# Opening of a hybrid RWKV-7 / HGRN2 step: clearings moved from GpSimd to VectorE, masks and norm scaling reordered

## The chip, the core and the metric

One core of a Trainium2 chip runs the whole program. The time is device microseconds of one launch, as a median over runs. A profiled execution adds a trace of every instruction: TensorE (PE, with its weight loads PEld), VectorE (DVE), ScalarE (ACT), GpSimd (POOL), SyncE (SP, which here issues the DMAs). Each engine takes its instructions in a fixed order, and an instruction waits for the semaphores of the ones whose results it needs; everything behind it on that engine waits with it.

## The reference, cut to what matters

One decoder layer serves 256 prompt tokens and 8 sequences of 8 sampled tokens, together 320 tokens of width 2048. The part that the change touches is the beginning:

```
h = x * rsqrt(mean(x*x) + eps) * norm_g        # rms_norm, 320 x 2048
p = h @ w_in                                   # 2048 -> 12416 columns
```

From p come the two branches: RWKV-7 (token shift, decay, a delta-rule matrix state for 16 heads) and HGRN2 (a gated linear recurrence for 8 heads, chunk by chunk). Each is projected back to 2048 columns, the two are merged by sigmoid gates computed from p, and an output projection, a residual add and a final norm follow. The states and shift rows are outputs too.

## The kernel before, in words

All large products are done in three passes. Each float32 operand is split in a high part (a cast to the fp32r type) and a low part (what is left), and high x high, low x high and high x low are summed in PSUM. The weights come in blocks of 1024 rows by 128 columns (512 KB, tile `raw`); ScalarE makes the high part `whi`, VectorE or GpSimd subtracts to make the low part `wlo`. There are three buffers of each, so a weight load (SyncE) must wait until the low part of the block three earlier has been taken. The result of one column tile is 128 columns x 320 tokens, 48 matmuls.

The kernel has four parts. The opening loads x, norms it, turns it to 16 tiles of 128 channels x 320 tokens and computes the first column tile of `p`. Then comes a long part whose instructions are recorded and put in an order by a planner with fixed costs (L1448 is the line that issues all of them), then the gates and projections, and the output projection. The change is in the opening alone.

The opening, as the code has it:

- x lies in three tiles `xt`: two of 128 prompt tokens and one of 64 sampled tokens (number 2, loaded first). `norm_g` is loaded as 4 rows of 512 (`gq`).
- Before the hand-ordered part GpSimd prepares constants: `ident`; `gr` and `sel`, which are cleared (L410, L411) and used to spread norm_g; `rows` (L417); the masks `lvs`, `lvz`, `seqm` (L449 to L463), `mk` (L468 to L474) and `mf` (L480 on). The masks are made by clearing and then cutting with affine selects (`keep_ge`, L437). L474 multiplies two 128 x 64 blocks of `mk` by `seqm`, and L494 copies `mf` four times as bytes into `mu8`.
- The rest stands in a part in which PE, ScalarE, VectorE and GpSimd take their instructions exactly as written. VectorE first fills `ones`, the `jr_...` matrices (L551 to L556), `yz`, `qz` and others (L563), `rs_a` and `rs_b`.
- norm_g is spread over 128 partitions: ScalarE casts `gq` into `gr` (L574), VectorE puts the rest in rows 32 to 35 (L575), four matmuls of `sel` and `gr` (L578) give four banks of PSUM, and VectorE copies them into `gb` (L579). VectorE then clears `arp` (L580).
- `warm(n)` issues n matmuls whose result nobody uses (L541).
- For each x tile, ScalarE sums the squares (`squares`, L502) and makes the factor (`scale`, L507 and L508). VectorE multiplies x by factor and norm_g (`gain`, L513) in pieces of 512 or 1024 columns. PE transposes (`turn`, L525) into one of six PSUM buffers, ScalarE takes the high part (`high`, L529), VectorE the low part (`low`, L533), which sets the buffer free.
- `first(part, k4)` issues four matmuls of one of the three passes of the first column tile (L612). `half(b, hf)` splits half of a weight block, ScalarE the high part (L618), GpSimd the low part (L619). `divide` splits a whole one (L401, L402).
- SyncE loads weight block 0 again as soon as `half(0, 1)` is done, block 1 after `half(1, 1)`, block 2 after `divide(2, 1, G)` (all L395).
- At the end ScalarE copies `seq4` and `lvz` (L671 to L673). The first instructions of the planned part then read the first tile's result (`pad`), run the decay's low-rank input through exponentials, and split the weights `wst` and `ast` of a small product that PE needs early.

Of the kernel before, what the change touches and what calls it, by code (L numbers as in the profile page):

```python
# [9 lines left out]
F32 = mybir.dt.float32  # L10
# [284 lines left out]
def hybrid_step(ctx, tc, x_prompt, x_sample, state_rwkv, state_hgrn, state_shift, norm_g, w_in,  # L295
# [4 lines left out]
    V, S, G, T = nc.vector, nc.scalar, nc.gpsimd, nc.tensor  # L300

    S.add_instruction(mybir.InstLoadActFuncSet(
        name=nc.get_next_instruction_name(), act_func_set_id=EXP_LN_SET, ins=[], outs=[]))
# [11 lines left out]
    def ctile(shape, name, dt=F32, pool=rconst):  # L315
        return pool.tile(shape, dt, name=name, tag=name)
# [17 lines left out]
    HS = [slice(0, 64), slice(64, 128)]  # L334
# [41 lines left out]
    with tc.tile_pool(name="start", bufs=1) as st, \  # L376
            tc.tile_pool(name="pst", bufs=6, space=PSUM) as pst:
        gq = st.tile([4, 512], F32, name="gq")
        nc.sync.dma_start(gq, norm_g.rearrange("o (r c) -> (o r) c", c=512))
        gb = st.tile([128, D], F32, name="gb")  # L380
# [17 lines left out]
        def divide(b_, n, sub):  # L398
            for j in range(n):
                ks = slice(8 * j // n, 8 * (j + 1) // n)  # L400
                S.copy(whi[b_][:, ks], wraw[b_][:, ks])  # L401
                sub.tensor_sub(wlo[b_][:, ks], wraw[b_][:, ks], whi[b_][:, ks].bitcast(F32))  # L402
            return whi[b_], wlo[b_]
# [3 lines left out]

        gr = st.tile([64, 512], F32R, name="gr")
        sel = st.tile([64, 4, 128], F32R, name="sel")
        G.memset(gr.bitcast(F32), 0.0)  # L410
        G.memset(sel.bitcast(F32), 0.0)  # L411
        for h in range(2):
            sl = slice(32 * h, 32 * h + 32)
            G.affine_select(out=sel[sl], in_=sel[sl], pattern=[[-1, 4], [0, 128]],
# [29 lines left out]
        low_ = HS[0]  # L444
        lvs = st.tile([128, 5, 32], F32, name="lvs")
        lvz = ctile([128, 5, 2, 32], "lvz")
        seqm = ctile([128, NSEQ], "seqm")
        mk_lv = {}
        G.memset(lvs[low_], 1.0)  # L449
        G.memset(seqm[low_], 1.0)  # L450
        for n, sz in enumerate((2, 4, 8, 16, 32)):
            mk_lv[sz] = lvz[:, n]
# [5 lines left out]
        keep_ge(seqm[low_], [[8, 8]], 7, -1)  # L458

        seq4 = ctile([128, 4], "seq4")  # L460
        G.memset(lvz[low_, :, 1], 0.0)
        G.memset(lvz[HS[1], :, 0], 0.0)
        G.tensor_copy(seqm[HS[1]], seqm[low_])  # L463

        mk = ctile([128, 3, 2, 64], "mk")
        G.memset(mk[:, 0:2], 1.0)  # L468
        for c_ in range(2):
            for sl in HS:  # L470
                keep_ge(mk[sl, c_], [[1, 2], [1, 64]], -1, -1)
# [6 lines left out]
        mf = st.tile([32, 3, 32], F32, name="mf")  # L478
        mu8 = ctile([128, 3, 32], "mu8", U8)
        G.memset(mf, 1.0)  # L480
        for n, sz in enumerate((8, 8, 16)):
# [8 lines left out]
            G.memset(lv[:, :, 0, :], 0.0)  # L490
            keep_ge(lv[:, :, 1, :], [[-2 * sz, nb], [0, sz]], 0, 1)
            keep_ge(lv[:, :, 1, :], [[2 * sz, nb], [0, sz]], sz - 1, -1)
        for g in range(4):
            G.tensor_copy(mu8[32 * g:32 * g + 32], mf)  # L494

        junk = st.tile([128, D], F32, name="junk")
        ssq = [st.tile([128, 2], F32, name=f"ssq{j}") for j in range(3)]

# [11 lines left out]
        def gain(j, k4, w=1):  # L510
            xt, n = xts[j]
            cs = slice(512 * k4, 512 * (k4 + w))
            V.scalar_tensor_tensor(xt[:n, cs], xt[:n, cs], ssq[j][:n, 0:1], gb[:n, cs], op0=ALU.mult, op1=ALU.mult)  # L513
# [13 lines left out]
        def high(j, k4):  # L527
            _, ks, tok = span(j, k4)
            S.copy(hhi[:, ks, tok], tps[j, k4])  # L529

        def low(j, k4):
            _, ks, tok = span(j, k4)
            V.tensor_sub(hlo[:, ks, tok], tps[j, k4], hhi[:, ks, tok].bitcast(F32))  # L533
# [5 lines left out]
        def warm(n):  # L539
            for _ in range(n):  # L540
                T.matmul(wps[:, :256], ones[:, :128], ones, start=True, stop=True)  # L541

        tps = {}
        with tc.manual_schedule(engines={mybir.EngineType.PE, mybir.EngineType.Activation, mybir.EngineType.DVE,
                                        mybir.EngineType.Pool}):
            ones = st.tile([128, 256], F32R, name="ones")
            V.memset(ones.bitcast(F32), 1.0)

            jr_sum, jr_mean, jr_cent, jr_all = (ctile([128, 128], n, F32R)
                                                for n in ("jr_sum", "jr_mean", "jr_cent", "jr_all"))  # L550
            V.memset(jr_all.bitcast(F32), 1.0 / 128.0)  # L551
            for t_, x in ((jr_sum, 1.0), (jr_mean, 1.0 / 64.0)):
                V.memset(t_.bitcast(F32), 0.0)
                for sl in HS:
                    V.memset(t_[sl, sl].bitcast(F32), x)
            V.tensor_sub(jr_cent, ident, jr_mean.bitcast(F32))  # L556

            yz = ctile([128, 2, 2, 2, 64], "yz")
            yd = ctile([128, 2, 2, 64], "yd")
            qz = ctile([128, NSEQ, 32], "qz")  # L560
            arp = ctile([128, 5, 2, 2, 64], "arp")
            for t_ in (yz, qz, lora_lw[HS[1]].bitcast(F32), lora_la[HS[0]].bitcast(F32)):
                V.memset(t_, 0.0)  # L563


            rs_a = ctile([128, NT], "rs_a")
            rs_b = ctile([128, NT], "rs_b")
            V.memset(rs_a, 1.0)
            V.memset(rs_a[:, 0:NP_:64], 0.0)
            V.memset(rs_a[:, NP_::8], 0.0)  # L570
            V.memset(rs_b, 1.0)
            V.memset(rs_b[:, ::8], 0.0)

            S.copy(gr[0:4], gq)  # L574
            V.tensor_sub(gr[32:36], gq, gr[0:4].bitcast(F32))  # L575
            for c_ in range(4):
                ps = pst.tile([128, 512], F32, name="gps", tag="t")
                T.matmul(ps, sel[:, c_], gr, start=True, stop=True)  # L578
                V.tensor_copy(gb[:, 512 * c_:512 * c_ + 512], ps)  # L579
            V.memset(arp, 0.0)  # L580
            warm(16)
            squares(2)
            scale(2)
            gain(2, 0, 2)
            turn(2, 0)
            warm(3)
            gain(2, 2, 2)
            turn(2, 1)
            warm(4)
            squares(0)  # L590
            scale(0)
            gain(0, 0, 2)
            turn(0, 0)
            turn(0, 1)
            squares(1)
            scale(1)
            gain(0, 2, 2)
            gain(1, 0)
            turn(1, 0)
            gain(1, 1)  # L600
            turn(1, 1)
            high(2, 0)
            high(0, 0)
            low(2, 0)
            low(0, 0)
            first_ps = psm.tile([128, 512], F32, name="mps", tag="m")

            def first(part, k4):

                w, x = ((whi, hhi), (whi, hlo), (wlo, hhi))[part]  # L610
                for k_ in range(4 * k4, 4 * k4 + 4):
                    T.matmul(first_ps[:, :NT], w[k4 // 2][:, k_ % 8], x[:, k_], start=part == 0 and k_ == 0,  # L612
                             stop=part == 2 and k_ == KT - 1)

            def half(b_, hf):

                ks = slice(4 * hf, 4 * hf + 4)
                S.copy(whi[b_][:, ks], wraw[b_][:, ks])  # L618
                G.tensor_sub(wlo[b_][:, ks], wraw[b_][:, ks], whi[b_][:, ks].bitcast(F32))  # L619

            half(0, 0)
            high(1, 0)
            low(1, 0)
            first(0, 0)
            gain(1, 2)
            gain(1, 3)
            half(0, 1)
            high(2, 1)
            high(0, 1)
            high(1, 1)  # L630
            low(2, 1)
            low(0, 1)
            low(1, 1)
            turn(0, 2)
            first(0, 1)
            turn(1, 2)
            first(1, 0)
            first(2, 0)
            half(1, 0)
            high(0, 2)  # L640
            high(1, 2)
            low(0, 2)
            low(1, 2)
            turn(0, 3)
            turn(1, 3)
            first(0, 2)
            first(1, 1)
            first(2, 1)
            half(1, 1)
            fetch(0, 0, 1)  # L650
            high(0, 3)
            high(1, 3)
            low(0, 3)
            low(1, 3)
            first(1, 2)
            first(2, 2)
            divide(2, 1, G)
            ps = pst.tile([128, 512], F32, name="cps", tag="t")
            T.transpose(ps[:, :128], rows, ident)
            V.tensor_copy(cols, ps[:, :106])  # L660
            ps = pst.tile([128, 512], F32, name="sps", tag="t")
            for j in range(2):
                T.transpose(ps[:, 100 * j:100 * j + 100], ssr[:, j], ident[:100, :100])
            V.tensor_copy(sst.rearrange("p s r -> p (s r)"), ps[:, :200])
            for part in range(3):
                first(part, 3)
            fetch(1, 1024, 0)
            divide(0, 1, G)
            fetch(2, 1024, 1)
            for j in range(4):  # L670
                S.copy(seq4[32 * j:32 * j + 32], seqm[0:32, 0:4])  # L671
            S.copy(lvz[HS[1], :, 1], lvs[low_])
            S.copy(lvz[low_, :, 0], lvs[low_])  # L673
# [766 lines left out]
    with tc.manual_schedule():  # L1440
# [3 lines left out]
        V, S, G, T, Y = (book.proxy(e) for e in ("V", "S", "G", "PE", "Y"))  # L1444
        record_all()
        V, S, G, T = real
# [193 lines left out]
```

## Time and profile before

| | us |
|---|---|
| median of three runs (1122.93 to 1124.36) | 1123.26 |
| profiled execution | 1123.37 |
| its span, first to last instruction | 1121.7 |
| PE busy | 1102.8 |
| VectorE busy | 761.6 |
| ScalarE busy | 693.1 |
| GpSimd busy | 192.8 |
| first matmul of the planned part (L1448) starts at | 28.98 |

A matmul's end is modelled and matmuls overlap, so PE's busy time is not a measure of PE at its peak. Starts of instructions are better for comparing: where a matmul of 320 columns follows another, they start 0.15 us apart. In rows of the order of time, instructions of one kind that follow each other closely are one row with a count; a row's length is then from the first start to the last end. Spans on GpSimd are rough.

### The profile page before, as it was taken

The numbers are of one execution on the slowest core, as the hardware profiler recorded it, in microseconds if no ns is written. First come the engines' busy times: TensorE is split into PE (matmuls) and PEld (weight loads), VectorE is DVE, ScalarE is ACT, GpSimd is POOL, SyncE is SP. The second block draws the span as 40 slices with busy tenths as digits, with TensorE's granted clock in tenths as the row PEclk, the third lists the DMA queues.
The fourth block names the chain that finished last, engine by engine and source line by source line (L and its number), as shares of the span: only waits on it lengthen the run. The fifth ranks groups of instructions, "written<-read, shape, count | busy, mean of one in ns | idle before, by whom it ended". The sixth has DMA issues, their size and how long they took to land.

```text
span 1121.7 us, 23666 instructions
## 1 busy us (share of the span) xinstructions
PE 1102.8 (98%) x9240; PEld 1066.6 (95%) x9240; DVE 761.6 (68%) x1625; ACT 693.1 (62%) x1572; POOL 192.8 (17%) x411
## 2 busy tenths in 40 slices
PE   6999999999999999999999999999999999999997
PEld 6999999999999999999999999999999999998886
DVE  8778888887887887887887876444444444437532
ACT  6777777677778678677776876444444444435422
POOL 9531231221311411412412200000000000000000
PEclk9999999999999999999999999999999999999998
DMA  6743545435435435435445354555555555587512
GB/s 178 201 132 107 152 117 146 137 98 155 128 96 158 131 105 165 133 96 163 124 124 145 97 144 138 150 150 150 151 149 151 150 151 150 151 269 242 187 33 93
DMA packets 283107, 159.87 MB, mean 143 GB/s; under 512 B 22893, under 2 KB 273264, under 8 KB 282356
## 3 DMA queue, kind: packets, MB, share of 16 engines
q1 hardware_dynamic: 282628, 157.06, 49.0%
q8 instruction: 72, 1.18, 0.4%
q10 hardware_dynamic: 368, 1.31, 0.4%
q14 instruction: 39, 0.32, 0.1%
HBM read 148.53 MB, written 9.81 MB: 141 GB/s over the span
## 4 chain that ended last, share of the span: by engine, by line
PE 94%; POOL 2%; ACT 2%; issue 1%; DVE 1%; DMA 1%; DVEq 0%; ACTq 0%; POOLq 0%
PE mps L1448 41%; PE a L1448 10%; PE mps L361 6%; PE mps L359 6%; PE mps L360 6%; PE b L1448 3%; PE po L1535 3%; PE po L1534 3%; PE po L1533 3%; PE ppa L359 2%; PE ppb L361 2%; PE ppb L359 2%; PE ppa L361 2%; PE ppb L360 2%; PE ppa L360 2%; PE y L1448 1%
## 5 line engine op out<-in xcount | busy, mean ns | idle before, releaser
L1448 PE MATMUL mps<-hhi,whi 128*128 128x320 f32 x1088 | 344.6, 317 | 0.0
L1448 PE MATMUL mps<-hlo,whi 128*128 128x320 f32 x1088 | 344.0, 316 | 0.5 <-issue 0.5
L1448 PE MATMUL mps<-hhi,wlo 128*128 128x320 f32 x1088 | 343.5, 316 | 0.0
L1448 PEld LDWEIGHTS mps<-hhi,whi 128*128 128x128 f32 x1088 | 204.8, 188 | 3.6 <-issue 2.7
L1448 PEld LDWEIGHTS mps<-hlo,whi 128*128 128x128 f32 x1088 | 204.9, 188 | 1.1 <-issue 0.4
L1448 PEld LDWEIGHTS mps<-hhi,wlo 128*128 128x128 f32 x1088 | 204.8, 188 | 0.7
L349 ACT CAST whi<-raw 128x1024 fp32r<-128x1024 f32 x88 | 92.4, 1050 | 162.7 <-PE mps L360 107.3
L350 DVE TENSOR_TENSOR wlo<-raw,whi 128x1024 fp32r<-128x1024 f32 x88 | 107.9, 1226 | 125.0 <-ACT whi L349 124.8
L1448 DVE TENSOR_TENSOR wlo<-raw,whi 128x1024 fp32r<-128x1024 f32 x134 | 164.6, 1228 | 16.9 <-ACT whi L1448 15.5
L1448 ACT CAST whi<-raw 128x1024 fp32r<-128x1024 f32 x134 | 140.2, 1046 | 56.3 <-PE mps L1448 55.3
L359 PE MATMUL mps<-hhi,whi 128*128 128x320 f32 x448 | 138.4, 309 | 0.0
L360 PE MATMUL mps<-hlo,whi 128*128 128x320 f32 x448 | 138.4, 309 | 0.0
L361 PE MATMUL mps<-hhi,wlo 128*128 128x320 f32 x448 | 138.4, 309 | 0.0
L359 PEld LDWEIGHTS mps<-hhi,whi 128*128 128x128 f32 x448 | 84.1, 188 | 0.0
L360 PEld LDWEIGHTS mps<-hlo,whi 128*128 128x128 f32 x448 | 84.1, 188 | 0.0
L361 PEld LDWEIGHTS mps<-hhi,wlo 128*128 128x128 f32 x448 | 84.1, 188 | 0.0
L1522 DVE TENSOR_TENSOR wlo<-raw,whi 128x1024 fp32r<-128x1024 f32 x32 | 38.6, 1223 | 36.9 <-ACT whi L1521 36.7
L1521 ACT CAST whi<-raw 128x1024 fp32r<-128x1024 f32 x32 | 33.2, 1051 | 47.6 <-PE po L1538 22.2
L1448 POOL TENSOR_TENSOR vm<-v,seq 96x512 fp32r<-96x512 f32 x16 | 16.9, 1056 | 200.3 <-ACT uK L1448 152.4
L1535 PE MATMUL po<-wlo,mhi 128*128 128x512 f32 x128 | 50.0, 391 | 0.0
L1533 PE MATMUL po<-whi,mhi 128*128 128x512 f32 x128 | 50.0, 391 | 0.0
L1534 PE MATMUL po<-whi,mlo 128*128 128x512 f32 x128 | 50.0, 391 | 0.0
(439 smaller groups left out, 2244.6 us busy)
## 6 DMA issues: line engine op xcount, KB each, us to landing
raw<-in_w_in_dram SPq DMA_DIRECT2D x194, 512.0 KB
raw<-in_w_out_dram SPq DMA_DIRECT2D x32, 512.0 KB
raw<-in_proj_a_dram SPq DMA_DIRECT2D x16, 512.0 KB
raw<-in_proj_b_dram SPq DMA_DIRECT2D x16, 512.0 KB
s<-in_state_hgrn_dram SPq DMA_DIRECT2D x8, 512.0 KB
out_dram<-s SPq DMA_DIRECT2D x8, 512.0 KB
s<-in_state_rwkv_dram SPq DMA_DIRECT2D x8, 256.0 KB
out_dram<-s SPq DMA_DIRECT2D x8, 256.0 KB
```

The source lines that it names most:

```text
L349: S.copy(hi[:, ks], raw[:, ks])
L350: sub.tensor_sub(lo[:, ks], raw[:, ks], hi[:, ks].bitcast(F32))
L359: T.matmul(dst, hi[:, q, :], xhi[:, k, :], start=(k == 0), stop=False)
L360: T.matmul(dst, hi[:, q, :], xlo[:, k, :], start=False, stop=False)
L361: T.matmul(dst, lo[:, q, :], xhi[:, k, :], start=False, stop=(k == nk - 1))
L1448: o.fn(*o.args, **o.kw)
L1521: S.copy(hi, raw)
L1522: V.tensor_sub(lo, raw, hi.bitcast(F32))
L1533: T.matmul(pt, h, hi, start=first, stop=False)
L1534: T.matmul(pt, l, hi, start=False, stop=False)
L1535: T.matmul(pt, h, lo, start=False, stop=end)
```

## The change

- Six clearings go from GpSimd to VectorE: `gr`, `sel`, `lvs`, two halves of `lvz`, and `mk[:, 0:2]`.
- The four copies of `mf` into `mu8` go from GpSimd to VectorE, behind the last low parts of x and the split of weight block 2.
- The cast and subtraction that make `gr` go to the front of VectorE's and ScalarE's order, right behind `ones`; the four matmuls and the copies to `gb` go right behind `jr_cent`, ahead of the clearings of `yz` and the others. ScalarE does the first and third copy, VectorE the second and fourth.
- The clearing of `arp` goes from in front of the scaling to behind the copies into `mu8`.
- `warm(16)` becomes `warm(20)`.
- `gain(1, 2)` and `gain(1, 3)` go ahead of `low(2, 0)` and `low(0, 0)`, so that all eight pieces of scaling come before the first low part.

```diff
-        G.memset(gr.bitcast(F32), 0.0)
-        G.memset(sel.bitcast(F32), 0.0)
+        V.memset(gr.bitcast(F32), 0.0)
+        V.memset(sel.bitcast(F32), 0.0)
...
-        G.memset(lvs[low_], 1.0)
+        V.memset(lvs[low_], 1.0)
         G.memset(seqm[low_], 1.0)
...
-        G.memset(lvz[low_, :, 1], 0.0)
-        G.memset(lvz[HS[1], :, 0], 0.0)
+        V.memset(lvz[low_, :, 1], 0.0)
+        V.memset(lvz[HS[1], :, 0], 0.0)
         G.tensor_copy(seqm[HS[1]], seqm[low_])
...
-        G.memset(mk[:, 0:2], 1.0)
+        V.memset(mk[:, 0:2], 1.0)
...
-        for g in range(4):
-            G.tensor_copy(mu8[32 * g:32 * g + 32], mf)
...
             V.memset(ones.bitcast(F32), 1.0)
+
+            S.copy(gr[0:4], gq)
+            V.tensor_sub(gr[32:36], gq, gr[0:4].bitcast(F32))
...
             V.tensor_sub(jr_cent, ident, jr_mean.bitcast(F32))
+            for c_ in range(4):
+                ps = pst.tile([128, 512], F32, name="gps", tag="t")
+                T.matmul(ps, sel[:, c_], gr, start=True, stop=True)
+                (V.tensor_copy if c_ % 2 else S.copy)(gb[:, 512 * c_:512 * c_ + 512], ps)
...
-
-            S.copy(gr[0:4], gq)
-            V.tensor_sub(gr[32:36], gq, gr[0:4].bitcast(F32))
-            for c_ in range(4):
-                ps = pst.tile([128, 512], F32, name="gps", tag="t")
-                T.matmul(ps, sel[:, c_], gr, start=True, stop=True)
-                V.tensor_copy(gb[:, 512 * c_:512 * c_ + 512], ps)
-            V.memset(arp, 0.0)
-            warm(16)
+            warm(20)
...
             high(0, 0)
+            gain(1, 2)
+            gain(1, 3)
             low(2, 0)
             low(0, 0)
...
             first(0, 0)
-            gain(1, 2)
-            gain(1, 3)
             half(0, 1)
...
             divide(2, 1, G)
+            for g in range(4):
+                V.tensor_copy(mu8[32 * g:32 * g + 32], mf)
+            V.memset(arp, 0.0)
```

## The prediction

> **What bounds the kernel now.** I read the page first, for the engine that the span belongs to.
>
> ```profile
> PE 1102.8 (98%) x9240; PEld 1066.6 (95%) x9240; DVE 761.6 (68%) x1625; ACT 693.1 (62%) x1572; POOL 192.8 (17%) x411
> PE 94%; POOL 2%; ACT 2%; issue 1%; DVE 1%; DMA 1%; DVEq 0%; ACTq 0%; POOLq 0%
> ```
>
> PE holds 94% of the chain that ended last; the rest is 67 us at most, and the change touches only the first 30 us. So the second view is the list of PE's waits from 29 us to the end, to see whether time saved in the opening can be lost again. These are its two longest rows:
>
> ```profile
> PE a L1448 <- DVE ast L1448: 0.8, 1, 0.8
> PE a L1448 <- DVE pp L1448: 0.7, 2, 0.3
> ```
>
> After 29 us PE waits next to never. Whatever moves the start of its steady stream moves the end by as much, and the first row, one wait of 0.8 us at 38 us, can add to that. The question is therefore when the stream of L1448 starts. The third view is the order of time of the opening, engine by engine (start, length, line, operation, tiles, count; in brackets the idle time and who ended it). VectorE:
>
> ```profile
> 0.93 0.27 DVE L547 MEMSET ones<- 128x256 f32 x1 [0.93 <-PEq L1628]
> 1.18 0.17 DVE L551 MEMSET jr_all<- 128x128 f32 x1
> 2.52 0.68 DVE L556 TENSOR_TENSOR jr_cent<-ident,jr_mean 128x128 fp32r<-128x128 f32 x1
> 3.27 0.48 DVE L563 MEMSET yz<- 128x512 f32 x1
> 5.81 0.09 DVE L572 MEMSET rs_b<- 128x40 f32 x1
> 5.94 0.68 DVE L575 TENSOR_TENSOR gr<-gq,gr 4x512 fp32r<-4x512 f32 x1
> 7.56 2.48 DVE L579 COPY gb<-gps 128x512 f32<-128x512 f32 x4 [0.95 <-PE gps L578]
> 10.26 1.12 DVE L580 MEMSET arp<- 128x1280 f32 x1 [0.22 <-issue]
> 11.31 6.14 DVE L513 SCALAR_TENSOR_TENSOR xt<-xt,ssq,gb 64x1024 f32<-64x1024 f32 x6
> 17.37 1.87 DVE L533 TENSOR_TENSOR hlo<-tps,hhi 128x512 fp32r<-128x512 f32 x3
> 19.17 1.40 DVE L513 SCALAR_TENSOR_TENSOR xt<-xt,ssq,gb 128x512 f32<-128x512 f32 x2
> 27.23 0.27 DVE L660 COPY cols<-cps 128x106 f32<-128x106 f32 x1 [1.57 <-PE cps L659]
> ```
>
> ScalarE and PE:
>
> ```profile
> 2.46 0.62 ACT L574 CAST gr<-gq 4x512 fp32r<-4x512 f32 x1 [0.37 <-DMA gq<-in_norm_g_dram]
> 6.42 1.91 ACT L502 ACTIVATE junk<-xt 64x2048 f32<-64x2048 f32 x1 [3.35 <-DMA xt<-in_x_sample_dram]
> 8.78 0.20 ACT L508 ACTIVATE ssq<-ssq 64x1 f32<-64x1 f32 x1
> 13.80 0.20 ACT L508 ACTIVATE ssq<-ssq 128x1 f32<-128x1 f32 x1
> 13.91 0.57 ACT L529 CAST hhi<-tps 128x512 fp32r<-128x512 f32 x1
> 27.85 1.05 ACT L401 CAST whi<-raw 128x1024 fp32r<-128x1024 f32 x1 [2.08 <-DMA raw<-in_w_in_dram]
> 30.30 0.38 ACT L1448 COPY pad<-mps 128x256 f32<-128x256 f32 x1
> 6.76 2.04 PE L578 MATMUL gps<-gr,sel 64*128 64x512 f32 x4 [6.76 <-DVE gr L575]
> 8.74 3.78 PE L541 MATMUL wps<-ones 128*128 128x256 f32 x16
> 14.66 0.74 PE L541 MATMUL wps<-ones 128*128 128x256 f32 x4
> 20.15 0.85 PE L612 MATMUL mps<-hhi,whi 128*128 128x320 f32 x4 [0.69 <-ACT hhi L529]
> 22.42 0.86 PE L612 MATMUL mps<-hhi,wlo 128*128 128x320 f32 x4 [0.40 <-POOL wlo L619]
> 24.57 0.75 PE L612 MATMUL mps<-hlo,whi 128*128 128x320 f32 x4
> 25.16 0.75 PE L612 MATMUL mps<-hhi,wlo 128*128 128x320 f32 x4
> 28.98 0.31 PE L1448 MATMUL mps<-hhi,whi 128*128 128x320 f32 x1
> ```
>
> GpSimd, and the longest wait of the DMA queue on SyncE:
>
> ```profile
> 1.01 0.52 POOL L410 MEMSET gr<- 64x512 f32 x1
> 2.44 1.32 POOL L414 TENSOR_SCALAR_AFFINE_SELECT sel<-sel 32x512 fp32r<-32x512 f32 x2
> 7.50 0.23 POOL L462 MEMSET lvz<- 64x160 f32 x1
> 7.93 0.30 POOL L468 MEMSET mk<- 128x256 f32 x1
> 10.04 6.20 POOL L474 TENSOR_TENSOR mk<-mk,seqm 128x64 f32<-128x64 f32 x2
> 18.44 2.56 POOL L494 CAST mu<-mf 32x96 uint8<-32x96 f32 x4
> 21.09 5.04 POOL L619 TENSOR_TENSOR wlo<-raw,whi 128x512 fp32r<-128x512 f32 x4
> SPq L395 <- POOL wlo L619: 9.0, 2, 7.0
> ```
>
> Two chains meet in PE. VectorE does the norm gains (L513) without a break from 11.31, although ScalarE had the first statistic at 8.98 (8.78 + 0.20): the gains wait behind memsets, the spread of norm_g (L575 to L579) and arp. GpSimd, busy 17% of the span, is late as well: its first low part starts at 21.09, right behind the mu8 copies, PE waits for it at 22.42, and SyncE's next weight load waits 7.0 us for the second.
>
> **The change, step by step.**
>
> *Memsets to VectorE.* Durations by width from VectorE's own rows: 512 wide 0.48 (yz), 256 wide 0.27 (ones), 128 wide 0.17 (jr_all). gr, sel, lvs, two halves of lvz and mk are then 2 x 0.48 + 3 x 0.2 + 0.27 = 1.8 us, from 0.93 to 2.75, if they stand first as the code has them; ones ends at 3.0. The cast of gr ends at 3.08 (2.46 + 0.62), so nothing is added: the DMA of norm_g covers them. Without that cover they cost up to 1.8.
>
> *Spread of norm_g.* The subtraction runs 3.1 to 3.8 in place of 5.94 to 6.62. sel is clear at 1.95, and its two selects take 1.32, to about 3.3 on GpSimd, so they fit too. PE starts 0.14 behind the subtraction as now: 3.9, four done at 5.95. VectorE meanwhile does jr_all to jr_cent, 2.03 us (1.18 to 3.20), until 5.8, then its two copies at some 0.6 each, to 7.05. ScalarE has no row for such a copy; its cast of the same tile is nearest, 0.57, and a VectorE copy is 2.48/4 = 0.62, so the pair ends near 6.05. The squares of x_sample wait for their DMA until 6.42: a margin of 0.35.
>
> *Start of the gains.* yz to rs_b, 2.63 us (3.27 to 5.90), now stand between: 7.05 + 2.63 = 9.7. arp's 1.12 is gone from here. The gains begin at 9.7 instead of 11.31, 1.6 us earlier. The third statistic (14.00) is needed at 14.4, so ScalarE does not hold them. The 20 warm-up matmuls, at 3.78/16 = 0.24 each, run from 5.95 to 10.7; the first transposes want 10.85. Hidden by 0.15, and being late there would cost nothing at once, since the next operands come 1.2 us apart.
>
> *All gains first.* Eight gains take 6.06 + 1.32 = 7.38 back to back, until 17.1; the first low part ends at 17.8. The six PSUM buffers of the opening all hold transposes by then, so turn(0,2) waits for that low part, then first(0,1). The other way to first(0,1) is gain(1,0), its transpose and the high parts on ScalarE, all 1.6 us earlier: 20.15 - 1.6 = 18.5. Both arrive near 18.4, so putting gains ahead costs nothing here; with the old order PE could have had the buffer 1.4 us sooner and used none of it.
>
> *GpSimd.* Taken off before mk: gr and sel 0.5 each, lvs and lvz 0.2 each three times, mk 0.27, less some 0.35 of waiting for sel: mk's two products start near 8.6 instead of 10.04. What they cost there the trace doesn't show. At their old price, 6.20, plus the 2.2 up to the mu8 copies (16.24 to 18.44), GpSimd is free at 17.1 and, at 1.26 for a low part (5.04/4), delivers the first at 18.4 and the second at 19.6. At best, below 1 us for both products before the gains begin, it is free by 12. At worst they are held until the last gain, 17.1, and with 0.6 and 2.2 and 1.3 the first low part comes at 21.1. I take the old price: same operation, same neighbours on VectorE. PE asks for that low part at about 20, so the wait at 22.42 (about 0.6 on PE from the end of the matmuls before it) goes.
>
> The Trainium skill (SBUF — State Buffer, Who interferes with whom) says that VectorE with two SBUF inputs excludes a GpSimd instruction that reads SBUF, and that a memset does not. By it the products finish in the memsets before 9.7. The row of mk, still running 4.96 us after it began beside an idle VectorE and a memset, is no support. Either way the sum is the same, as GpSimd has time to spare.
>
> *Stream start.* PE is then without a break from 18.5. Today 20.15 to 28.98 is 8.83, less 0.6 of waiting 8.2: 18.5 + 8.2 = 26.7, a gain of 2.3. The low half of the next weights needs two more casts and one 2.4 us subtraction, all ahead of 26.7 as GpSimd runs three microseconds earlier.
>
> *mu8 and arp* land in the gap before cols, 1.57 now. arp is 1.12. A byte copy on VectorE has no row in the opening; GpSimd's is 2.56/4 = 0.64, VectorE's smallest memset 0.09, so four are 0.4 to 2.6, and I take 0.8. Together 1.9, up to 0.4 late at cols, whose readers come after the stream's start; nothing on PE.
>
> *The wait at 38 us.* The first tile's results are done near 29.1, but ScalarE copies pad only at 30.30, behind a weight cast that waited 2.08 for a load that SyncE could issue only after the second low part (23.6; it came 4.2 later). With the second low part at 19.6, load, cast and the 2.45 us up to pad (27.85 to 30.30) end at 23.8 + 2.45 = 26.3, before 26.8, when the tile is done. The lag of 1.2 goes, and with it most of the 0.8 us wait on ast; a weight cast on ScalarE in between is tied to PE's pace, so I count 0.7 (0 to 0.8).
>
> **Sum:** 2.3 + 0.7 = 3.0. The profiled execution is 1123.37 with a span of 1121.7, 1.7 outside it unchanged; 1123.37 - 3.0 = 1120.4, and as it lies 0.1 over the median of the runs, 1120.3.
>
> **Rivals.**
> 1. *The wait at 38 us stays* (its chain is long and meets PE-paced weight casts): 1123.3 - 2.3 = 1121.0. For: ast's row is only the last link. Against: the lag at pad goes.
> 2. *GpSimd is no earlier*, the masks do not get ahead of the scaling: first low part at 21.1, PE waits 1.0, the load is late and the 38 us wait stays: 2.3 - 1.0 = 1.3, 1122.0. For: mk's 6.20. Against: two products ended inside the gains.
> 3. *VectorE is held by GpSimd.* With a faster GpSimd its first low part becomes ready near 15.6, among the gains, and holds one of them 1.26: 3.0 - 1.2 = 1.8, 1121.5. For: nothing but order. Against: the 6.14 for six gains while mk was pending shows no gap. The Trainium skill (SBUF — State Buffer, SBUF: two separate sides) says that whoever starts first keeps the shared ports for a whole instruction, which would be this case; the row of the gains does not bear it out.
> 4. *The moved work queues in front of ScalarE*: memsets placed behind jr, say, make sel and gr 2 us late, the copies push the squares by 1.65 and the third statistic to 15.65, past 14.4: 3.0 - 1.25, 1121.6.
> 5. *Slower: PE's clock drops.* A warm-up matmul costs 0.24 at first; later four take 0.74, so PE doubles its pace after a busy stretch. If the 20 run fast near their end they stop about 8.6, 2.2 us before the first transposes, and PE could fall back. Four matmuls of the first tile take 0.59 (24.57 to 25.16), twelve groups 7.1; at half pace 7.1 more: 1120.3 + 7.1 = 1127.4. It decides once 3.0/7.1, or 42%, of them run slowly. Against: PE idles 6.7 us at the start today, none so long after.
>
> **How the numbers follow.** Less than 0.2% (2.2 us) can't be told from no change here, so faster means under 1121.0. Forecast 0.55, at 1120.3, own range 1119.6 to 1121.0; rival 1 0.13, rival 2 0.12, rival 3 0.08, rival 4 0.07, rival 5 0.05. The low end 1119.4 adds what a GpSimd at best and the whole 0.8 can give, with run scatter; the high end 1122.3 takes in rivals 1 to 4. Faster: nearly all of the forecast and half of rival 1, 0.60; slower 0.06 with rival 5 and some scatter; same 0.34.
>
> **What would show it.** gps near 3.9 and gains from 9.7; no wait of PE for wlo; first low part between 17 and 20; L1448's first matmul near 26.7; pad right behind it; no wait on ast. A gap inside the gains, a squares row later than 6.5, first low parts after 20.5 or matmul groups over 1 us would prove a rival.

## The result, and the profile after

The changed kernel takes 1125.54 us (median of ten runs, 1122.63 to 1127.4), the kernel before 1123.36 in the same comparison (ten runs, 1122.6 to 1124.36). The ratio is 1.0018 with an interval of 1.001 to 1.0026: slower by 0.2%, where 1120.3 was forecast and slower had a chance of 0.06. The profiled execution of the changed kernel is 1125.08, its span 1123.4, 1.7 more than before. Line numbers move with the edit: L1447 is the planned part (L1448 before), L510 the gains, L530 and L526 the low and high parts of x, L617 and L402 GpSimd's low parts of the weights, L655 the copies into `mu8`, L656 `arp`.

First the page: busy times of the engines, and the shares of the chain that ended last.

```profile
PE 1104.9 (98%) x9244; PEld 1069.0 (95%) x9244; DVE 766.6 (68%) x1633; ACT 693.6 (62%) x1574; POOL 188.1 (17%) x401
PE 94%; DVE 3%; ACT 2%; issue 1%; DMA 0%; SPq 0%; DVEq 0%; ACTq 0%
```

PE is still the bound. What is new is VectorE's 3% on the chain (1% before) in place of GpSimd's 2%. The order of time of the opening (start, length, engine, line, operation, tiles, count; in brackets the idle time before it and who ended it) has the rows that answer to those of before:

```profile
3.28 0.68 DVE L547 TENSOR_TENSOR gr<-gq,gr 4x512 fp32r<-4x512 f32 x1
9.60 8.55 DVE L510 SCALAR_TENSOR_TENSOR xt<-xt,ssq,gb 64x1024 f32<-64x1024 f32 x8
24.05 5.22 DVE L655 CAST mu<-mf 32x96 uint8<-32x96 f32 x4
29.60 1.12 DVE L656 MEMSET arp<- 128x1280 f32 x1 [0.33 <-issue]
30.64 0.20 DVE L659 COPY cols<-cps 128x106 f32<-128x106 f32 x1
6.78 1.91 ACT L499 ACTIVATE junk<-xt 64x2048 f32<-64x2048 f32 x1 [0.43 <-DMA xt<-in_x_sample_dram]
29.42 0.37 ACT L1447 COPY pad<-mps 128x256 f32<-128x256 f32 x1 [2.96 <-issue]
31.30 0.21 ACT L1447 ACTIVATE lbt<-lbt 128x8 f32<-128x8 f32 x1 [1.50 <-DVE lbt L1447]
4.11 2.04 PE L559 MATMUL gps<-gr,sel 64*128 64x512 f32 x4 [4.11 <-DVE gr L547]
27.36 0.31 PE L1447 MATMUL mps<-hhi,whi 128*128 128x320 f32 x1
38.75 0.38 PE L1447 MATMUL a<-lora_a,ast 128*128 128x320 f32 x1 [3.15 <-DVE ast L1447]
8.42 0.55 POOL L474 TENSOR_TENSOR mk<-mk,seqm 128x64 f32<-128x64 f32 x2
15.87 4.66 POOL L617 TENSOR_TENSOR wlo<-raw,whi 128x512 fp32r<-128x512 f32 x3
29.40 0.48 SPq L1447 DMA_DIRECT2D w2a<-in_rwkv_w_dram  x1
```

The opening did what it should: norm_g is spread from 4.11, the gains start at 9.60, GpSimd's low parts at 15.87, and the stream of the planned part starts at 27.36, 1.6 us earlier than before. But the four copies into `mu8` take 5.22 us, and what stands behind them is late. SyncE's load of `w2a` starts when the last copy is through (29.27), and the list of the DMA queue's waits names VectorE's `mu` for it; ScalarE's `pad` starts at the same moment, though its row names nothing that it waited for ("issue"). Both are still 0.9 earlier than in before (30.30). What comes later than in before is `cols`, at 30.64 instead of 27.23, and what is computed from it: ScalarE waits 1.50 for VectorE's `lbt` and starts on it at 31.30, where before had it at

```profile
30.57 0.21 ACT L1448 ACTIVATE lbt<-lbt 128x8 f32<-128x8 f32 x1
```

ScalarE's next weight cast, VectorE's subtraction of that block, the exponentials and at last `ast` stand behind it in the engines' order, and each is 0.7 later than in before. PE's list of waits has grown in one row, from 0.8 before:

```profile
PE a L1447 <- DVE ast L1447: 3.2, 1, 3.2
```

The product that reads `ast` starts at 38.75. In before it is this row of the order of time:

```profile
38.02 0.39 PE L1448 MATMUL a<-lora_a,ast 128*128 128x320 f32 x1 [0.82 <-DVE ast L1448]
```

It is 0.7 later now: the 1.6 us of the opening are gone, and more. The wait has grown by both, 1.6 and 0.7. The order of time with one instruction per row shows what stretched the copies. The first and last of the four take 0.2 each; these are the two between, and GpSimd's two subtractions of the block split:

```profile
24.26 2.43 DVE L655 CAST mu<-mf 32x96 uint8<-32x96 f32 x1
26.70 2.35 DVE L655 CAST mu<-mf 32x96 uint8<-32x96 f32 x1
24.23 2.40 POOL L402 TENSOR_TENSOR wlo<-raw,whi 128x1024 fp32r<-128x1024 f32 x1 [1.24 <-ACT whi L401]
26.59 2.40 POOL L402 TENSOR_TENSOR wlo<-raw,whi 128x1024 fp32r<-128x1024 f32 x1
```

Each long copy starts just behind a subtraction and ends just behind it. Then the wait itself has a cost beyond its length. The table by stretches (length; busy time of PE, PEld, VectorE, ScalarE and GpSimd, each with its count of instructions; then PE's granted clock, DMA share and GB/s):

```profile
35.60:39.01 3.41, 0.26 (x2) 0.29 (x3) 2.25 (x6) 3.24 (x10) 2.11 (x6) 1.00 1.21 292
39.01:42.42 3.41, 3.41 (x15) 3.37 (x15) 2.62 (x5) 2.70 (x6) 3.30 (x12) 0.50 0.60 142
42.42:46.00 3.58, 3.58 (x27) 3.58 (x26) 2.28 (x9) 3.21 (x9) 0.30 (x2) 1.00 0.51 146
```

PE was busy for 0.26 of the first 3.41 us, and from 39.01 it ran 3.41 us at half its clock: 15 matmuls where the next 3.58 us hold 27. In before the clock stays at 1.00 there. From the starts of the same matmuls in both kernels, the account in us (after minus before) is -1.6 at the start of the stream, +0.7 at the product that reads `ast`, +2.2 when the clock is back at 42.4 (1.47 from the half pace), and +1.7 at the end; the last step is a pause of 0.5 near 490 us that this execution doesn't have.

### The profile page after: what moved, and what is told of

It is laid out like the page before. It is cut to its first block, busy times and chain, and to the rows that moved or that the text cites. A ratio compares the mean times of both kernels' runs of the same rounds, so it can differ in the third digit from the quotient of the medians.

```text
span 1123.4 us, 23675 instructions
## 1 busy us (share of the span) xinstructions
PE 1104.9 (98%) x9244; PEld 1069.0 (95%) x9244; DVE 766.6 (68%) x1633; ACT 693.6 (62%) x1574; POOL 188.1 (17%) x401
## 4 chain that ended last, share of the span: by engine, by line
PE 94%; DVE 3%; ACT 2%; issue 1%; DMA 0%; SPq 0%; DVEq 0%; ACTq 0%
PE mps L1447 41%; PE a L1447 10%; PE mps L359 6%; PE mps L360 6%; PE mps L361 6%; PE b L1447 3%; PE po L1534 3%; PE po L1533 3%; PE po L1532 3%; PE ppa L360 2%; PE ppb L360 2%; PE ppa L359 2%; PE ppb L359 2%; PE ppb L361 2%; PE ppa L361 2%; PE y L1447 1%
## 5 line engine op out<-in xcount | busy, mean ns | idle before, releaser
L1447 PE MATMUL mps<-hhi,whi 128*128 128x320 f32 x1088 | 344.9, 317 | 0.0
L1447 PE MATMUL mps<-hlo,whi 128*128 128x320 f32 x1088 | 344.6, 317 | 0.0
L1447 PE MATMUL mps<-hhi,wlo 128*128 128x320 f32 x1088 | 344.1, 316 | 0.0
L1447 PEld LDWEIGHTS mps<-hhi,whi 128*128 128x128 f32 x1088 | 205.1, 188 | 3.6 <-issue 2.7
L1447 PEld LDWEIGHTS mps<-hlo,whi 128*128 128x128 f32 x1088 | 205.3, 189 | 1.1 <-issue 0.4
L1447 PEld LDWEIGHTS mps<-hhi,wlo 128*128 128x128 f32 x1088 | 205.3, 189 | 0.7
L1447 DVE TENSOR_TENSOR wlo<-raw,whi 128x1024 fp32r<-128x1024 f32 x134 | 164.6, 1228 | 17.2 <-ACT whi L1447 15.8
L1447 ACT CAST whi<-raw 128x1024 fp32r<-128x1024 f32 x134 | 140.0, 1046 | 55.8 <-PE mps L1447 54.7
L1447 POOL TENSOR_TENSOR vm<-v,seq 96x512 fp32r<-96x512 f32 x16 | 16.8, 1051 | 200.2 <-ACT uK L1447 130.0
```

The costliest lines, as they stand in the source:

```text
L1447: o.fn(*o.args, **o.kw)
```

## The experiments

Where an expectation names a theory by a letter: **A** says that a copy or cast on VectorE and a subtraction on GpSimd exclude each other, so that one waits for the other to end; **A'** says that any VectorE instruction from SBUF to SBUF would be held so; **B** says that the place matters, since copies and `arp` queue in front of `cols` whatever they cost; **C** says that the clock lost after the wait is a part of the loss; **E**, formed later, says that PE's clock, which comes up late in the opening, is behind the loss and the scatter of the kernel before with its copies on ScalarE, and perhaps behind part of the changed kernel's better opening. The brackets behind a time hold its lowest and highest run, those behind a ratio its 95% interval. In each comparison the kernel before ran beside, with 1122.9 to 1123.0 as its median.

### The copies on ScalarE, same place

```diff
-                V.tensor_copy(mu8[32 * g:32 * g + 32], mf)
+                S.copy(mu8[32 * g:32 * g + 32], mf)
```

> The changed kernel, with the four byte copies into mu8 done by ScalarE at the same place in the order instead of VectorE. Theory A (in the changed kernel two of VectorE's copies take 2.43 and 2.35 us because they and GpSimd's 2.40 us low-part subtractions exclude each other; that makes cols late and with it ast, PE waits 3.2 us and then runs at half pace for about 3 us): copies of about 0.25 us each on ScalarE, cols right behind arp near 26, the wait of PE on ast under 0.5 us, no half pace, 1120.5 to 1121.5 us, at least 2 us under the kernel before. Rival B (arp's 1.12 us and the longer queue of VectorE in front of cols are what is late): cols still behind arp, ScalarE's tail 1 us later, a wait of 1.5 us or more on ast stays, 1123 or above.

Measured: 1119.79 (1119.63 to 1120.13), 0.9973 [0.9962, 0.9984]. The row of the tile `mu` (shortest, median and longest in ns), then the order of time:

```profile
L655 ACT CAST mu<-mf x4: 262/268/272, 23.3 to 24.2; 32x96 uint8<-32x96 f32 x4
```

```profile
24.91 0.27 DVE L659 COPY cols<-cps 128x106 f32<-128x106 f32 x1 [0.23 <-PE cps L658]
26.93 0.38 ACT L1447 COPY pad<-mps 128x256 f32<-128x256 f32 x1
26.66 0.31 PE L1447 MATMUL mps<-hhi,whi 128*128 128x320 f32 x1
34.88 0.39 PE L1447 MATMUL a<-lora_a,ast 128*128 128x320 f32 x1
```

`cols` comes 2.3 us earlier than before and `pad` 3.4. The product that reads `ast` starts at 34.88 without a wait, 3.1 earlier than before, and the median is 3.2 below before. With this one word changed the kernel is the fastest of all here; it gains a little more than had been forecast for the change (3.0), and lies below the range that was expected of this edit.

### The copies on VectorE as a reduction

`tensor_reduce` over an axis of length one computes the same bytes; engine, place and queue stay.

```diff
-                V.tensor_copy(mu8[32 * g:32 * g + 32], mf)
+                V.tensor_reduce(mu8[32 * g:32 * g + 32], mf[:, :, :, None], axis=mybir.AxisListType.X, op=ALU.max)
```

> The changed kernel, with the four byte copies still on VectorE at the same place, written as a maximum over an axis of length one (tensor_reduce) instead of a copy: same engine, queue, bytes and order. Theory A, if what excludes GpSimd is the copy's fast mode that uses the second read port: four of 0.15 to 0.35 us, cols at 26 to 26.5, no wait on ast above 0.5 us, 1120.5 to 1121.5. Theory A', any VectorE instruction from SBUF to SBUF is held by GpSimd's subtraction: at least one copy of 2 us or more again, 1124 to 1126. Rival B (queue length): 1123 or above with short copies.

Measured: 1120.72 (1120.65 to 1120.8), 0.998 [0.9971, 0.9988]. The row of the tile, then the order of time:

```profile
L655 DVE TENSOR_REDUCE mu<-mf x4: 229/244/245, 23.3 to 24.0; 32x96 uint8<-32x96 f32 x4
```

```profile
23.53 4.81 POOL L402 TENSOR_TENSOR wlo<-raw,whi 128x1024 fp32r<-128x1024 f32 x2 [1.02 <-ACT whi L401]
26.02 2.35 DVE L1447 TENSOR_SCALAR neg<-cols 128x16 f32<-128x16 f32 x1
```

The reductions take 0.24 each, two of them beside GpSimd's subtraction (from 23.53). So theory A' falls: the form of the instruction decides, not that it runs on VectorE. A holds, and the second row shows it again: a `tensor_scalar` of 16 columns, 0.17 in the changed kernel, is now the one that meets GpSimd's second subtraction and takes 2.35. With that hold, and with `cols` at 25.63 behind the reductions, PE still waits 1.0 for `ast`, twice the 0.5 that was expected at most, and this kernel stays 0.9 behind the one with ScalarE; that much theory B can have at most.

The Trainium skill (SBUF — State Buffer, Who interferes with whom) states that VectorE and GpSimd share a pair of ports as an exclusive lock, that copy, cast and tensor_scalar can use it and tensor_reduce can't on this chip. The trace agrees on all: 2.43 and 2.35 for the casts, 2.35 for the tensor_scalar, 0.24 for the reductions.

### Work for PE during the wait

Twenty matmuls that nobody uses, into a tile that is overwritten next, stand ahead of the product that reads `ast`; the copies stay on VectorE.

```diff
...
+            if todo and o.eng == "PE" and o.args[1].tensor.name.startswith("ast"):
+                todo = False
+                for _ in range(20):
+                    T.matmul(o.args[0][:, :256], jr_all, hhi[:, 0, :256], start=True, stop=True)
```

> The changed kernel, with 20 matmuls of 256 columns added on PE directly ahead of the product that waits for ast (into its own output, which the first real matmul then starts anew). They last about 2.1 us and lie inside the wait. Theory C (about 1.5 us of the loss is PE's clock, which falls to half in the idle stretch of 3.3 us and takes 3.3 us to come back): the product still starts near 38.7, but matmuls behind it follow at 0.15 us instead of 0.27, 1123.5 to 1124.3 us, and the runs scatter less. Rival D (the slower pace behind the wait has another cause, weights or results that are late): pace stays at 0.27, 1125.5 as the changed kernel.

Measured: 1123.06 (1122.37 to 1123.68), 1.0001 [0.9992, 1.001]. Order of time, then a stretch of the table:

```profile
34.73 2.51 PE L1451 MATMUL a<-hhi,jr_all 128*128 128x256 f32 x20
37.76 0.41 PE L1452 MATMUL a<-lora_a,ast 128*128 128x320 f32 x1 [0.51 <-DVE ast L1452]
```

```profile
38.70:42.20 3.50, 3.50 (x27) 3.49 (x26) 2.35 (x5) 3.50 (x8) 3.04 (x13) 1.00 0.34 81
```

`ast` is as late as the copies make it (37.76), but the clock stays at 1.00 through 38.7 to 42.2, where the changed kernel had 0.50 for 3.41 us. The runs lie within 1.3 us, those of the changed kernel within 4.8. The time is below the 1123.5 to 1124.3 that was expected, as the stream starts at 26.66 in this execution. The fair partner is therefore the second execution of the changed kernel (further down), whose stream starts at 26.66 too and whose product starts at 37.84: its span is 1122.4, this one's 1121.1. Theory C holds: idle time of PE has a second price, of 1.3 to 1.5.

### The copies back on GpSimd, behind the masks

```diff
+        for g in range(4):
+            G.tensor_copy(mu8[32 * g:32 * g + 32], mf)
...
-            for g in range(4):
-                V.tensor_copy(mu8[32 * g:32 * g + 32], mf)
```

> The changed kernel, with the byte copies into mu8 back on GpSimd, behind the making of mf and ahead of the first low part; everything else of the change stays. Theory A: cols is early, no wait on ast above 0.8 us; GpSimd's copies start near 16 and two of them are held by VectorE's last gains, so its first low part comes at 19 to 20.5 and PE waits up to 0.7 us for it; stream start 27.3 to 28.2, time 1120.8 to 1122.3. Rival B: arp ahead of cols alone keeps the wait on ast at 1.5 us or more, 1123 or above.

Measured: 1120.24 (1119.58 to 1121.59), 0.9977 [0.9968, 0.9986]. The copies take 0.26 each from 17.6 to 18.7, and PE's wait on `ast` is 0.5. That is faster than expected, because no copy met a gain: the last gain ended at 17.1.

```profile
L494 POOL CAST mu<-mf x4: 255/259/262, 17.6 to 18.5; 32x96 uint8<-32x96 f32 x4
```

Undoing this one part of the change gives nearly all that the change was forecast to give. The four copies cost GpSimd 1.2 us, and the stream starts only 0.1 later than with them on ScalarE (26.74).

### The changed kernel once more

> The changed kernel once more, for a second profiled execution and more times. Theory A with C: again exactly two of the four byte copies on VectorE last above 2 us, since there are two subtractions of 2.40 us on GpSimd in that stretch, whichever copies they are; PE waits 2.5 to 3.5 us on ast and then issues matmuls 0.27 us apart for 2 to 8 us. Open: whether the last gain is held for 1 us again (1.76 us in the first profiled execution, 0.74 in those of the four kernels run since); if not, the stream of L1447 starts at 26.7 instead of 27.4. Time 1123 to 1127, scatter over 2 us.

Measured, unchanged: 1124.23 (1122.69 to 1127.98), 1.0013 [1.0004, 1.0022]. The order of time, for the last gain, and the table by stretches:

```profile
16.38 0.74 DVE L510 SCALAR_TENSOR_TENSOR xt<-xt,ssq,gb 128x512 f32<-128x512 f32 x1
```

```profile
37.70:41.11 3.41, 3.27 (x12) 3.30 (x13) 2.44 (x5) 2.45 (x6) 2.93 (x11) 0.50 0.68 164
```

Two copies are held again (four take 5.12), PE waits 3.0 for `ast`, and the clock halves for the same 3.41 us. One thing differs. In the first profiled execution the last gain was held too, by GpSimd's first low part (15.87 on):

```profile
16.38 1.76 DVE L510 SCALAR_TENSOR_TENSOR xt<-xt,ssq,gb 128x512 f32<-128x512 f32 x1
```

Here it took 0.74, GpSimd's low parts began at 17.49, and the stream started at 26.66 in place of 27.36. So who gets in first differs between executions of one program. In the four other profiled kernels with the same opening (copies on ScalarE, copies as a reduction, and both with matmuls during the wait) the last gain took 0.74 as well. The runs' own mean granted clocks go with their times: 0.997 in those of 1122.7, 0.996 around 1124.2, 0.995 at 1125.4 to 1125.8, 0.993 at 1127.98. One lost window, as I call 3.41 us at half pace, is 3.41 x 0.5 / 1122 = 0.0015, so the slowest run fits two to three of them (0.997 less 0.993); it has no trace. In the ten runs of the first comparison the order is less clear: 1125.87 has 0.993, and 1127.4 has 0.995.

### Two gains back behind a low part, copies on ScalarE

```diff
-            gain(1, 2)
-            gain(1, 3)
             low(2, 0)
...
             first(0, 0)
+            gain(1, 2)
+            gain(1, 3)
```

> The kernel with the byte copies on ScalarE, and gain(1,2) and gain(1,3) back behind low(1,0) in VectorE's order, as in the kernel before. The prediction held that putting them ahead costs nothing, since turn(0,2) and the high part for first(0,1) come at the same time: then first(0,1) still starts at 18.4 to 18.6 and the time is within 0.5 us of 1119.8. If the gains ahead cost what turn(0,2) waits today (0.41 us on PE), 0.3 to 0.5 us less; if they help by keeping VectorE's gains away from GpSimd's subtractions, a gain of over 1.5 us length appears and PE's wait for wlo comes back, 0.5 to 1.5 us more.

Measured: 1121.11 (1120.98 to 1121.29), 0.9983 [0.9975, 0.9992], 1.3 over the kernel with all gains first. Order of time:

```profile
17.52 3.40 DVE L510 SCALAR_TENSOR_TENSOR xt<-xt,ssq,gb 128x512 f32<-128x512 f32 x2
16.17 2.50 POOL L615 TENSOR_TENSOR wlo<-raw,whi 128x512 fp32r<-128x512 f32 x2
19.05 1.32 POOL L615 TENSOR_TENSOR wlo<-raw,whi 128x512 fp32r<-128x512 f32 x1 [0.38 <-ACT whi L614]
```

The two gains take 1.7 each in place of 0.74: they fall among GpSimd's low parts. first(0,1) starts at 18.50 in either order, so putting the gains ahead costs nothing there, as forecast. The loss comes behind it: the stream starts 0.6 later (27.30), and PE waits 0.8 for `ast` again. The wait for `wlo` that the expectation named does not come back. So putting all gains first is worth 1.3, and these rows have the reason: it takes them out of GpSimd's way.

### The six clearings back on GpSimd, copies on ScalarE

```diff
-        V.memset(gr.bitcast(F32), 0.0)
+        G.memset(gr.bitcast(F32), 0.0)
...            (and so with sel, lvs, two halves of lvz, mk)
```

> The kernel with the byte copies on ScalarE, and the six clearings back on GpSimd. Prediction's step: they free GpSimd about 1.5 us ahead of the mask products, and VectorE pays nothing as it waits for the cast of gr anyway. Theory A: the gains still start at 9.6; GpSimd comes to the products near 10, inside the gains, is held to their end at 17.1, and its first low part ends near 20 to 20.5, about when PE asks for it: 1119.8 to 1120.8 us. If the clearings carry the gain: 1121 or more.

Measured: 1120.43 (1120.23 to 1120.66), 0.9976 [0.9966, 0.9985], 0.6 over the kernel with them on VectorE.

```profile
11.28 6.44 POOL L474 TENSOR_TENSOR mk<-mk,seqm 128x64 f32<-128x64 f32 x2
18.92 1.27 POOL L617 TENSOR_TENSOR wlo<-raw,whi 128x512 fp32r<-128x512 f32 x1
```

`mk`'s products now meet the gains and are held 6.44 (0.55 in the changed kernel, at 8.42 among memsets), so the first low part comes at 18.92. PE doesn't wait for it in this trace. What the trace has of the 0.6 are a later spread of norm_g (from 4.34, behind `sel`), gains from 9.76 in place of 9.61, a stream from 26.84 in place of 26.66, and a wait of 0.3 for `ast`.

### The kernel before, with only the copies on ScalarE

```diff
-        for g in range(4):
-            G.tensor_copy(mu8[32 * g:32 * g + 32], mf)
...
             divide(2, 1, G)
+            for g in range(4):
+                S.copy(mu8[32 * g:32 * g + 32], mf)
```

> The kernel before, with nothing changed but the four byte copies, which ScalarE does behind the split of weight block 2. GpSimd starts its first low part at 18.4 instead of 21.1, PE's wait for it goes (0.6 us), the next weight load goes out near 21 instead of 23.65, pad is copied at about 28.9 instead of 30.30 and the wait on ast (0.8 us) goes: 1.2 to 1.5 us under the kernel before. If only the earlier start of the gains matters, no change (within 0.4 us).

Measured: 1124.94 (1123.13 to 1126.99), 1.0016 [1.0007, 1.0025]: not the gain expected, but slower. The order of time of one of its faster executions (1123.3):

```profile
20.57 2.44 DVE L511 SCALAR_TENSOR_TENSOR xt<-xt,ssq,gb 128x512 f32<-128x512 f32 x2
19.98 1.26 PE L610 MATMUL mps<-hhi,whi 128*128 128x320 f32 x4
21.97 0.85 PE L610 MATMUL mps<-hhi,whi 128*128 128x320 f32 x4 [0.28 <-ACT hhi L527]
```

Freed of the copies, GpSimd comes earlier to its low parts, and these now hold a gain (2.44 for two, 1.40 before). PE is also still at its lower pace at 19.98 (1.26 for four matmuls, 0.85 later), though the table by stretches prints a granted clock of 1.00 there; the first record of the clock in this trace is at 20.90. PE's wait for `ast` is gone, as expected, but the stream starts at 30.13, 1.15 later than in before. The times fall in three groups, near 1123.3, 1125.0 and 1126.8, whose mean granted clocks are 0.998, 0.996 to 0.997 and 0.995: by their size these may be lost windows again, but the slower ones have no trace.

### More warm-up matmuls: with that edit, and alone

Both kernels add 28 warm-up matmuls right behind `ones` and have 30 for 16 later.

```diff
             V.memset(ones.bitcast(F32), 1.0)
+            warm(28)
...
-            warm(16)
+            warm(30)
```

> The kernel before with its byte copies on ScalarE, which scatters from 1123.1 to 1127.0 in groups some 1.7 us apart and whose trace has PE's clock at half until 20.9 us, and 28 warm-up matmuls more right at the start (PE is idle there until 6.8) and 30 instead of 16 later. Theory E (that kernel's loss and scatter are PE's clock, which comes up at one of several times 3.4 us apart, as the busy stretch before the first transposes is only 5.8 us): clock at full before 9 us in the trace, scatter under 1 us, 1121.3 to 1122.0 us. Rival F (the loss comes from moving the copies to ScalarE, by its longer tail in front of pad): 1123 or above, scatter as before.

> The kernel before with the same additional warm-up matmuls and nothing else. Theory E: the kernel before has its clock at full at 13.3 us in the one trace there is, a little late for the transposes; little to gain, 1122.0 to 1122.9 us. If part of the changed kernel's better opening is only its earlier warm-up, 1121.5 or less.

Measured: with the copies on ScalarE 1123.59 (1123.05 to 1125.64), 1.0006 [0.9997, 1.0015]; alone 1123.29 (1122.84 to 1124.06), 1.0001 [0.9992, 1.001]. Warm-up alone brings nothing, so theory E doesn't explain the changed kernel's opening. For the kernel with its copies on ScalarE it is half right: the warm-up takes 1.35 off (1124.94 to 1123.59) and a third of the scatter, but the time stays outside the 1121.3 to 1122.0 that E gave. The profiled execution of this kernel is one of the three slow ones among eleven (1125.43; eight lie between 1123.05 and 1124.09). Its order of time, then the table by stretches:

```profile
18.94 4.33 DVE L511 SCALAR_TENSOR_TENSOR xt<-xt,ssq,gb 128x512 f32<-128x512 f32 x2
18.33 3.73 POOL L618 TENSOR_TENSOR wlo<-raw,whi 128x512 fp32r<-128x512 f32 x3
22.71 1.08 PE L523 MATMUL tps<-ident,xt 128*128 128x128 f32 x4 [1.98 <-issue]
```

```profile
18.82:22.23 3.41, 1.22 (x8) 0.72 (x6) 3.41 (x2) 2.01 (x5) 3.23 (x3) 1.00 0.25 76
22.23:25.64 3.41, 2.93 (x12) 2.96 (x13) 3.41 (x7) 1.10 (x2) 0.63 (x1) 0.50 0.50 145
```

One gain, between three of GpSimd's low parts, is held until 22.6; PE idles nearly 2.0 us, and the next 3.41 us run at half pace. So in both traces, in the old order of gains, a GpSimd freed of the copies collides with VectorE. That speaks for the collision as the reason why moving the copies alone does not pay; what it costs apart from PE's low pace, and whether it happens in the eight faster executions, which have no trace, stays open.

### Eight matmuls during the wait

As with twenty above, but eight.

> The changed kernel with 8 instead of 20 matmuls ahead of the product that waits for ast: about 0.9 us of the 3.0 to 3.3 us are filled, some 2.1 us of idle time are left in a row. If the clock falls only when nearly a whole window of 3.4 us is idle (it fell with 2.9 and 3.3, not with 0.9): no half pace, 1122.8 to 1123.4 as with 20, scatter under 1.5 us. If half a window is enough: part of the runs 1.7 us longer, median 1123.5 to 1125 and scatter over 2 us.

Measured: 1123.97 (1121.7 to 1124.44), 1.0003 [0.9994, 1.0012]. Median and scatter are those expected if half a window of idle time is enough for the clock to fall. The profiled execution, the one of 1121.7, can't show it:

```profile
23.26 2.96 DVE L655 CAST mu<-mf 32x96 uint8<-32x96 f32 x4
23.53 2.41 POOL L402 TENSOR_TENSOR wlo<-raw,whi 128x1024 fp32r<-128x1024 f32 x1 [1.03 <-ACT whi L401]
26.07 2.42 POOL L402 TENSOR_TENSOR wlo<-raw,whi 128x1024 fp32r<-128x1024 f32 x1
```

Here only one copy is held: the second subtraction starts at 26.07, after the last copy has begun. The four copies take 2.96 in place of 5.12 to 5.22, and `cols` comes at 27.59. The eleven times fall into one of 1121.7, four of 1122.5 to 1122.8 and six of 1124.0 to 1124.4. Read with the traces above, these would be one copy held, two held, and two held with a lost window (the last two 1.5 apart); they have no trace of their own, so this reading is not shown.

## Why the prediction was wrong, step by step

- **Memsets, spread of norm_g, start of the gains**: right. gps at 4.11 (3.9 forecast), gains at 9.60 (9.7). The squares came at 6.78, past the 6.5 that was to prove a rival, but behind their DMA: ScalarE's copies to `gb` had ended at 6.34.
- **GpSimd**: the first low part was to start at 17.1 and be done at 18.4. It ran from 15.87 to 17.60 in the first execution and from 17.49 to 18.76 in the second, inside the range. That this is so near is luck. The old price of `mk` was the wrong choice: 0.55 against 6.20. I set the rule of the Trainium skill (SBUF — State Buffer, Who interferes with whom) aside because one row, `mk` running beside an idle VectorE and a memset, seemed to speak against it; by that rule the products finish among the memsets, and they did. What was held instead were the pieces of `mf` behind them, among the gains: five selects from 9.56 to 15.87, one of them 3.60, about as much as `mk` was to cost. Why the first product of before took 4.96, though it began ahead of the gains, stays open.
- **All gains first "costs nothing"**: right that it costs nothing (first(0,1) at 18.50 where no gain is held, forecast 18.5), but it is worth 1.3, for the reason that rival 3 named.
- **Stream start** 26.7: 26.66 in the second execution of the changed kernel; 27.36 in the first, where a gain was held for 1.76. That is rival 3, VectorE held by GpSimd, whose row I judged not to bear it out. It happened in one of the two profiled executions of the changed kernel, and in none of the four profiled kernels with the same opening.
- **`mu8` and `arp` land in the gap before `cols`, "nothing on PE"**: the step that failed, in both halves. First the cost: I took 0.8 for four copies, at most 2.6, from VectorE's smallest memset and the mean of GpSimd's copies, 0.64. Measured were 5.1 to 5.2, as two of the copies stood still for one GpSimd subtraction each (3.0 where only one did). The rows to see it by were there: the mean of 0.64 hides three copies of 0.26 and one of 1.65, which ran beside the two late gains (the row below; shortest, median and longest in ns). I also placed a 2.4 us subtraction of GpSimd near that stretch in the paragraph before, and rival 3 had the mechanism, but I tried it on the gains alone. Then the reach: I held that the readers of `cols` cost PE nothing. `lbt` is one of them, and the work that leads to `ast` stands behind it, as the starts at 31.30 and 38.75 show. The row of GpSimd's copies in before:

```profile
L494 POOL CAST mu<-mf x4: 254/262/1650, 18.4 to 20.7; 32x96 uint8<-32x96 f32 x4
```

- **The wait at 38 us goes**: right once the copies are off VectorE (no wait on `ast`, 0.8 gained). With the copies as the change has them it grew to 3.2.
- **PE's clock (rival 5)**: the mechanism is real and cost 1.47 here, but not where I put it. The warm-up held; the clock fell after the new wait at 39 us. In the opening it fell only behind a long wait.
- **The sum**: 3.0 for opening and wait was the right size; with the copies on ScalarE 3.2 is measured (1122.98 less 1119.79), 2.3 of it at the start of the stream (28.98 to 26.66) and 0.8 at `ast`, as forecast. On VectorE the profiled execution of the changed kernel loses 5.3 against that one (1125.08 less 1119.79): 0.7 at the start of the stream, 3.2 at `ast`, 1.5 by the clock.

What stays open is how often each outcome occurs: which engine is first differs between executions, and only the profiled ones show it.

## What to carry to other kernels

Before an instruction is moved to VectorE because it is short, look at what GpSimd runs in that stretch: a cast or a tensor_scalar there, or an operation with two inputs from SBUF as the gains are, can cost as long as GpSimd's instruction (here 2.4 in place of 0.2), and all that queues behind it pays. Look also at the spread of a price, not only at its mean. A small move is better put on ScalarE, or in a form that doesn't meet GpSimd, and its readers on every engine are to be listed, not only the next in line. A new wait on PE of some 2 to 3 us is to be priced with another 1.5 for the clock: it fell behind idle stretches of 2.0, 3.0 and 3.2 here, and not behind those of 1.0 and 1.4 in these traces.

## What the runs showed of the hardware that was not expected

- A cast of 32 x 96 elements, 0.19 to 0.2 alone on VectorE, took 2.33 to 2.43 beside a 2.40 us subtraction on GpSimd; a gain of 0.74 took 1.7 to 1.8 beside one low part of 1.26, and in one case two gains took 4.33 beside three. The same bytes cost 0.24 as a reduction, 0.27 on ScalarE, 0.26 on GpSimd when nothing held it; beside the gains one of GpSimd's own copies took 1.65.
- The order in which the two engines get in is not fixed: the same program held a gain or none, and with the same instructions up to 34 us one copy was held instead of two.
- PE's clock halves for 3.41 us at a time, which costs about 1.5 (1.47 behind the wait for `ast`). The Trainium skill (TensorE: Matmul & The Clock Gate, What's actually happening) gives a window of that length and half rate after an idle window. The trace agrees on length and rate. But the window need not be wholly idle: PE was busy for 1.22 us of the 3.41 before the fall at 22.23, by ends that are modelled.
